# A two-layer decoder trunk on one core: program head reordered, attention outputs stored as split pairs, whole inputs re-read from DRAM, last attention later

## The chip, the core and the metric

One core of a Trainium2 chip runs the whole program in one launch. The engines have their own queues and run them strictly in order: PE (matrix products), DVE (vector), ACT (scalar activations, casts, and some DMA issues), POOL and SP (here mostly DMA issues). The time is the device time of the core in microseconds, median over runs. All data are float32.

## The reference, cut to what matters

Two residual layers over 512 tokens of width 2048. Layer 0 is gated differential attention, layer 1 is RWKV-7 time mixing; the change touches layer 0 alone, and the place where layer 1's first projection starts is not touched.

```python
hn = rms_norm(x, norm_w[0])
q, k, v, gate = jnp.split(hn @ w_in, 4, axis=-1)          # 8 heads, q and k: 2 x 128, v: 256
q = apply_rope(rms_norm(q, q_gain), cos, sin)
k = apply_rope(rms_norm(k, k_gain), cos, sin)
a = softmax(q0 k0) - lam * softmax(q1 k1)                 # causal, blocks of 128 queries
o = rms_norm(a @ v, subln_w) * (1.0 - lambda_init)
x = x + (o * silu(gate)) @ w_out
```

## The kernel before, in words

**Products in pairs.** A float32 operand is split into a high part (rounded to fp32r) and a low part (the rest), and a product is three fp32r products: high by high, high by low, low by high (`mm3`, L122). Weights are loaded as `wraw` tiles of 128x2x512 (512 KB); ACT casts the high part `wh` (L105), DVE subtracts for the low part `wl` (L106). The activations are kept transposed: `hH[k]`, `hL[k]`, 128 channels by 512 tokens, k from 0 to 15.

**Head 0** is computed plainly: `unit_tok` runs over eight weight pairs of 24 matmuls each, first for q and k (`qk0`), then for v and gate. While q and k of head 0 are computed, `make_h` (L1042, L1043) turns the rows of xT into `hH` and `hL` with the norm's weight; the token-wise factor 1/rms is applied later, to q, k and v. For that factor, ACT squares x (tile `junkx`, L822, 16 times 128x512, with sums), and DVE adds and takes the reciprocal root (`rsqrt`, lines 64 to 71). `copy_out` (L249) moves the four accumulators of `qk0` to the tiles `t1`; `head_qk` (L261 to L280) norms and rotates them; `turn_qk` (L295 to L299) transposes them in a chain of small steps.

**Heads 1 to 7** use a seven-product scheme on 2x2 blocks (`unit_head`, L544), for which `input_sums` prepares sums and differences of the halves of `h` once, during the v/gate unit of head 0 (S1, S2, S4) and after it (S3). Weight sums Ta, Tb, Tc are made by DMAs on POOL that accumulate into a loaded tile. The attention of head h-1 is cut into steps (a `Chain`) and put between the matmuls of head h, some matmuls apart; its output is transposed (`yt`, L387), scaled (L393) and stored to `yd` in DRAM (L394).

**The output projection** reads the attention outputs back as rows: `split_rows` loads rows 0 to 13 into the t1 tiles (`yr`, L441, on SP), ACT casts (L431) and DVE subtracts (L432). Rows 14 and 15 come straight from the attention of head 7, which is interleaved with the first of the projection's two plain column blocks. The other two column blocks use the seven-product scheme again.

**What sets the order.** The program is written in one order and a scheduler fixes the queue of every engine when the program is built: an instruction gets a priority from its place, `high_priority` moves it ahead, `issue_after` holds it until another one is placed. Nothing is reordered when it runs: what stands at the head of an engine's queue and waits, holds all that stand behind.

Of the kernel before, what the change touches and what calls it, by code (L numbers as in the profile page):

```python
# [34 lines left out]
class Ctx:  # L35
    pass

# [208 lines left out]
def copy_out(g, dst, ps):  # L246
    with g.tc.high_priority(offset=AHEAD):
        for d, p in zip(dst, ps):
            g.nc.scalar.copy(d, p[:])  # L249
# [76 lines left out]
def attention(g, h, qkT, qkL, sq, V, VL, G, gap, rows=None, keys=()):  # L326
# [57 lines left out]
    def turn_y(t):  # L384
# [5 lines left out]
        if rows is None:  # L390
            yT = w.tile([P, 2, P], F32, name="yTh", tag="yTh", bufs=1)
            for c in range(2):
                nc.scalar.activation(yT[:, c], pv[:, c], AF.Copy, scale=g.subw[:, c : c + 1])  # L393
            nc.scalar.dma_start(out=g.yd[h * 256 : (h + 1) * 256, ts].rearrange("(c p) t -> p c t", p=P), in_=yT[:])  # L394
            return
# [57 lines left out]
def input_sums(g, late):  # L453
# [301 lines left out]
def layer0(g, aps):  # L755
    nc, tc = g.nc, g.tc
    lx = ExitStack()
    g.lc = lx.enter_context(tc.tile_pool(name="lc0", bufs=1))
    with ExitStack() as cx:
# [76 lines left out]
        with tc.issue_after(g.made[-1][0]), tc.issue_after(g.made[-1][1]), tc.issue_after(masked):  # L836
# [5 lines left out]
    with ExitStack() as cx:  # L842
        g.work = cx.enter_context(tc.tile_pool(name="work", bufs=2))
        before = None
        for h in range(NH):
            if h:
                Chain(g, attention(g, h - 1, *before, 28 if h > 1 else 26, keys=rest), 20)
            t1s = [g.work.tile([P, 512], F32, name="t1", tag="t1", bufs=4) for _ in range(NT)]
# [12 lines left out]
            else:  # L861
                copy_out(g, [t[:] for t in t1s], qk0)
# [843 lines left out]
```

## Time and profile before

| | us |
|---|---|
| runs | 2154.02, 2154.74, 2157.23 (median 2154.74) |
| profiled execution, its own time | 2149.57 |
| its span, first to last instruction | 2147.8 |
| PE busy in it | 2107.1 (98%) |
| DVE, ACT, POOL busy | 1601.3 (75%), 1135.1 (53%), 361.6 (17%) |
| mean granted PE clock | 0.993 |

In the rows of a timeline the first number is the start, the second the busy time, then engine, line, operation, tiles and shapes; in brackets the idle time of the engine ahead of it and what ended it. In a table of windows each engine's busy time comes with the number of its instructions, then the granted PE clock, the share of the DMA engines that was busy, and GB/s.

### The profile page before, as it was taken

Reading aid. Unit: us, or ns where it says so; the run is one execution under the profiler, and the core shown is the slowest. Engines: PE = TensorE matmul, PEld = TensorE weight load, DVE = VectorE, ACT = ScalarE, POOL = GpSimd, SP = SyncE. Lnnn points to the kernel's source line nnn. Section 1 sums busy time; section 2 is a strip of 40 time slices with the busy share of each in tenths; the row PEclk is TensorE's granted clock in tenths of the full one; section 3 lists DMA queues with packets and bytes.
Section 4 is the critical chain, followed back from the end, with each engine's and each line's share of the span. In section 5 each row is a group of like instructions: output and inputs, shape, how many; then the busy total and the mean of one; then the engine's idle time right before and its main releaser. Section 6 shows DMA issues by size and latency. Waiting matters only on the chain.

```text
span 2147.8 us, 34089 instructions
## 1 busy us (share of the span) xinstructions
PE 2107.1 (98%) x11936; PEld 1712.8 (80%) x11936; DVE 1601.3 (75%) x4087; ACT 1135.1 (53%) x2265; POOL 361.6 (17%) x729
## 2 busy tenths in 40 slices
PE   9999999999999999999999999999999999999999
PEld 7788888888888788878676888788887887877887
DVE  5897888878788885575777778877777788766645
ACT  5565555655555453355554555565555555644322
POOL 1010101011011100101222222222222222221001
PEclk9999999999999999999999999999999999999999
DMA  8567767677676656723222322322332223336555
GB/s 273 142 140 180 167 156 180 156 186 157 167 186 162 175 193 195 173 76 105 79 79 77 94 84 92 93 89 87 94 96 92 89 87 95 111 115 186 178 164 120
DMA packets 132893, 288.32 MB, mean 134 GB/s; under 512 B 47232, under 2 KB 57472, under 8 KB 132720
## 3 DMA queue, kind: packets, MB, share of 16 engines
q1 hardware_dynamic: 75648, 187.46, 27.1%
q0 software_dynamic: 22048, 76.20, 18.5%
q10 hardware_dynamic: 35024, 22.46, 3.3%
q8 instruction: 94, 1.54, 0.3%
q14 instruction: 79, 0.65, 0.1%
HBM read 266.09 MB, written 19.99 MB: 133 GB/s over the span
## 4 chain that ended last, share of the span: by engine, by line
PE 69%; DVE 19%; issue 4%; DMA 4%; ACT 2%; POOL 0%; SPq 0%; ACTq 0%; DVEq 0%; POOLq 0%
PE pp L122 29%; PE pp L544 21%; PE pt L122 5%; DVE wl L106 4%; DVE tmpl L1305 3%; DVE Tm L1307 2%; DVE VS L1440 1%; PE sc L122 1%; PE gp L1241 1%; PE sm L1418 1%; DMA td<-Tm 1%; PE lora L122 1%; PE sm L1436 1%; DMA x<-in_x_dram 1%; PE o L122 1%
## 5 line engine op out<-in xcount | busy, mean ns | idle before, releaser
L106 DVE TENSOR_TENSOR wl<-wraw,wh 128x1024 fp32r<-128x1024 f32 (+2 forms) x305 | 371.3, 1217 | 233.1 <-ACT wh L105 220.1
L105 ACT CAST wh<-wraw 128x1024 fp32r<-128x1024 f32 (+2 forms) x305 | 318.3, 1044 | 342.9 <-PE pp L122 173.3
L122 PE MATMUL pp<-hH,wl 128*128 128x512 f32 x1024 | 415.4, 406 | 0.2 <-DVE wl L106 0.2
L122 PE MATMUL pp<-hL,wh 128*128 128x512 f32 x1024 | 415.2, 406 | 0.0
L122 PE MATMUL pp<-hH,wh 128*128 128x512 f32 x1024 | 412.7, 403 | 0.0
L122 PEld LDWEIGHTS pp<-hH,wh 128*128 128x128 f32 x1024 | 194.4, 190 | 35.9 <-issue 1.8
L122 PEld LDWEIGHTS pp<-hL,wh 128*128 128x128 f32 x1024 | 194.1, 190 | 34.9
L544 PE MATMUL pp<-wh,hH 128*128 128x512 f32 x560 | 220.8, 394 | 0.0
L122 PEld LDWEIGHTS pp<-hH,wl 128*128 128x128 f32 x1024 | 194.4, 190 | 33.1 <-DVE wl L106 0.7
L544 PE MATMUL pp<-wh,hL 128*128 128x512 f32 x560 | 218.7, 391 | 0.0
L544 PE MATMUL pp<-wl,hH 128*128 128x512 f32 x560 | 174.8, 394 | 0.1
L122 PE MATMUL pp<-wh,hH 128*128 128x512 f32 x372 | 147.5, 398 | 8.1 <-ACT t L249 3.3
L122 PE MATMUL pp<-wl,hH 128*128 128x512 f32 x372 | 148.0, 400 | 2.4 <-DVE wl L106 2.4
L122 PE MATMUL pp<-wh,hL 128*128 128x512 f32 x372 | 148.0, 399 | 0.2
L1305 DVE SCALAR_TENSOR_TENSOR tmpl<-LT,Tm 128x60 f32<-128x60 f32 (+24 forms) x496 | 134.8, 272 | 10.9
L1424 POOL COPY SA<-VS 64x64 f32<-64x64 f32 x224 | 60.9, 272 | 457.4 <-DVE VS L1440 354.9
L544 PEld LDWEIGHTS pp<-wh,hL 128*128 128x128 f32 x560 | 105.3, 188 | 21.4
L544 PEld LDWEIGHTS pp<-wh,hH 128*128 128x128 f32 x560 | 105.2, 188 | 21.0
L544 PEld LDWEIGHTS pp<-wl,hH 128*128 128x128 f32 x560 | 103.1, 188 | 21.9 <-DVE wl L106 0.8
L1307 DVE TENSOR_TENSOR Tm<-Tm,tmpl 128x60 f32<-128x60 f32 (+24 forms) x496 | 103.8, 209 | 11.2
L122 PEld LDWEIGHTS pp<-wh,hH 128*128 128x128 f32 x372 | 71.1, 191 | 24.0 <-ACT t L249 3.8
L1431 ACT COPY VS<-sm 64x64 f32<-64x64 f32 x256 | 52.7, 206 | 63.3 <-PE sm L1429 58.4
(384 smaller groups left out, 4233.9 us busy)
## 6 DMA issues: line engine op xcount, KB each, us to landing
wraw<-in_rw_w_in_dram SPq DMA_DIRECT2D x128, 512.0 KB
wraw<-in_da_w_in_dram SPq DMA_DIRECT2D x92, 512.0 KB
wraw<-in_da_w_out_dram SPq DMA_DIRECT2D x26, 512.0 KB
wraw<-in_rw_w_out_dram SPq DMA_DIRECT2D x26, 512.0 KB
Ta<-in_da_w_in_dram POOLq DMA_DIRECT2D x21, 512.0 KB, 5.4
Tb<-in_da_w_in_dram POOLq DMA_DIRECT2D x21, 512.0 KB, 5.9
Tc<-in_da_w_in_dram POOLq DMA_DIRECT2D x21, 512.0 KB, 5.8
wraw<-in_da_w_in_dram POOLq DMA_DIRECT2D x21, 512.0 KB, 5.4
```

The source lines that it names most:

```text
L105: a = nc.scalar.copy(hi[:, ks], raw[:, ks])
L106: d = nc.vector.tensor_sub(lo[:, ks], raw[:, ks], hi[:, ks].bitcast(F32))
L122: m = nc.tensor.matmul(out, a, b, start=s, stop=e, skip_group_check=skip)
L544: m = nc.tensor.matmul(out[t][:], x, wt[lo][:, k, :], start=first, stop=end and lo == 1 and k == KG - 1, skip_group_check=True)
L1241: m = nc.tensor.matmul(gp[h][:, i * P : (i + 1) * P], BK[r_, c0 + i, :, :], p.AR[r_, c0 + i, :, :], start=True, stop=True)
L1305: nc.vector.scalar_tensor_tensor(tt, LT[:, i : i + 1, i + 1 :].to_broadcast([P, s, n]), n2[:, i : i + 1], Tm[:, 0:s, i : i + 1].to_broadca ...
L1307: nc.vector.tensor_add(Tm[:, 0:s, i + 1 :], Tm[:, 0:s, i + 1 :], tt)
L1418: nc.tensor.matmul(sm[:, 0:P], both(p.G[:, c, 0]), both(VS[:, c]), start=True, stop=True)
L1424: nc.gpsimd.tensor_copy(p.SA[r_, c - 1, :], VS[r_, c, h, :])
L1431: nc.scalar.copy(VS[r_, c, h, :], sm[r_, P : P + C])
L1436: nc.tensor.matmul(sm[:, o : o + P], p.BKT[:, c, :], both(VS[:, c]), start=True, stop=True)
L1440: g.state = nc.vector.scalar_tensor_tensor(VS[r_, c + 1, h, :], s_, p.gam[r_, c : c + 1], Sg[r_, :], ALU.mult, ALU.add)
```

## The change

1. *Head 0.* The tiles `t1` get a pool of their own that outlives the program head, so `copy_out` of `qk0` is written right behind the q/k unit. The loads of x (four of 1 MB, on ACT's queue) are issued behind later rows of `make_h`, most squares behind the copies, and the computation of lambda too.
2. *Sums of the inputs.* `input_sums` no longer adds `hH+hL` on DVE. It loads the rows of xT once more (18 loads of 256 KB on POOL's queue) and applies the norm's weight in the operations that form the sums. The chain that transposes q and k of head 0 starts 104 matmuls on instead of 80.
3. *Attention outputs* are split when they are stored: per block of 128 channels a high part (ACT) and a low part (DVE), two stores per query block to `ys` instead of one to `yd`. Two DMAs on POOL per head form the whole values in `yd` from `ys`, one head later: a copy, then an accumulating one.
4. *Output projection.* Rows 0 to 13 are loaded from `ys` straight into `hH` and `hL` (28 loads of 256 KB on SP); L431 and L432 fall away there.
5. *Head 7.* Its v/gate ending has no raised priority any more, and its attention starts 16 matmuls after the unit's end instead of 4, with steps 20 instead of 21 matmuls apart.

```diff
+class Work:
+    def __init__(self, pool, heads):
+        self.pool, self.heads = pool, heads
+    def tile(self, *a, tag=None, **k):
+        return (self.heads if tag == "t1" else self.pool).tile(*a, tag=tag, **k)
...
         if rows is None:
-            yT = w.tile([P, 2, P], F32, name="yTh", tag="yTh", bufs=1)
             for c in range(2):
-                nc.scalar.activation(yT[:, c], pv[:, c], AF.Copy, scale=g.subw[:, c : c + 1])
-            nc.scalar.dma_start(out=g.yd[h * 256 : (h + 1) * 256, ts].rearrange("(c p) t -> p c t", p=P), in_=yT[:])
+                yT = w.tile([P, 2, P], F32R, name="yTh", tag=("yTh", "th")[c], bufs=1)
+                nc.scalar.activation(yT[:, 0], pv[:, c], AF.Copy, scale=g.subw[:, c : c + 1])
+                nc.vector.scalar_tensor_tensor(yT[:, 1], pv[:, c], g.subw[:, c : c + 1],
+                                               yT[:, 0].bitcast(F32), ALU.mult, ALU.subtract)
+                nc.scalar.dma_start(out=g.ys[2 * h + c, :, :, ts], in_=yT[:].bitcast(F32))
+            if h and t in (1, 3):
+                part, op = ((0, ALU.bypass), (1, ALU.add))[t // 2]
+                nc.gpsimd.dma_start(out=g.yd[(h - 1) * 256 : h * 256, :].rearrange("(c p) t -> c p t", p=P),
+                                    in_=g.ys[2 * h - 2 : 2 * h, :, part], accum_op=op)
             return
...
-    def whole(k, tag):
-        r = w.tile([P, T], F32, name="whole", tag=tag, bufs=1)
-        nc.vector.tensor_add(r[:], g.hH[k][:].bitcast(F32), g.hL[k][:].bitcast(F32))
+    def whole(r, k):
+        nc.gpsimd.dma_start(out=r, in_=aps["xT"][:, k])
         return r[:, 0:256], r[:, 256:512]
-    def put(nm, k, o, x, y, op):
-        nc.vector.tensor_tensor(out=o, in0=x, in1=y, op=op)
+    def put(nm, k, o, scale=1.0):
         hi, lo = g.sums[nm][k]
-        nc.scalar.copy(hi, o)
-        nc.vector.tensor_sub(lo, o, hi.bitcast(F32))
+        nc.scalar.activation(hi, o, AF.Copy, scale=scale)
+        nc.vector.scalar_tensor_tensor(lo, o, scale, hi.bitcast(F32), ALU.mult, ALU.subtract)
+    def mixed(o, x, scale, op):
+        nc.vector.scalar_tensor_tensor(o, x, scale, o, ALU.mult, op)
...
         if late:
-            a, b = whole(k, "a")
-            put("S3", k, b, a, b, ALU.subtract)
+            a, b = whole(w.tile([P, T], F32, name="whole", tag=("a", "at", "p0", "p1")[k % 4], bufs=1), k)
+            nc.vector.tensor_sub(a, a, b)
+            put("S3", k, a, norm(k))
             continue
-        (a, b), (c, d) = whole(k, "p0"), whole(k + NH4, "p1")
-        put("S1", k, d, b, d, ALU.subtract)
-        put("S2", k, d, d, a, ALU.subtract)
-        put("S4", k, c, c, d, ALU.add)
+        pair = w.tile([P, 2, T], F32, name="pair", tag=("V", "VL", "acc1", "G")[k % 4], bufs=1)
+        (a, b), (c, d) = whole(pair[:, 0], k), whole(pair[:, 1], k + NH4)
+        nc.scalar.activation(d, d, AF.Copy, scale=norm(k + NH4))
+        mixed(d, b, norm(k), ALU.subtract)
+        put("S1", k, d)
+        mixed(d, a, minus[:, k : k + 1], ALU.add)
+        put("S2", k, d)
+        nc.vector.scalar_tensor_tensor(c, c, norm(k + NH4), d, ALU.mult, ALU.add)
+        put("S4", k, c)
...
+        t1s = [t1_tile() for _ in range(NT)]
+        copied = copy_out(g, [t[:] for t in t1s], qk0)
...
-            with tc.issue_after(g.made[(2, 5, 8, 10)[cb]][0]):
+            with tc.issue_after(g.made[(7, 10, 13, 15)[cb]][0]):
...
-                with tc.issue_after(g.made[min(4 * cb + t + 6, KT - 1)][0]):
+                with tc.issue_after(g.made[12 + t][0] if cb == 0 else copied):
...
-                copy_out(g, [t[:] for t in t1s], qk0)
...
-                Chain(g, keys(NT), 80)
-                input_sums(g, False)
+                Chain(g, keys(NT), 104)
+                input_sums(g, aps, False)
...
-            with tc.high_priority(offset=AHEAD if h == NH - 1 else 0):
-                before = qkT + (sq,) + head_vg(g, h, vg, G)
+            before = qkT + (sq,) + head_vg(g, h, vg, G)
...
-        rows = split_rows(g, g.yd, ("t1",), 4, KT - 2, 8, g.gated)
-        ch = Chain(g, attention(g, h, *before, 21, rows, rest), 4)
+        rows = []
+        for k in range(KT - 2):
+            rows.append([g.hp.tile([P, T], F32R, name=n, tag=n) for n in ("hH", "hL")])
+            for i in range(2):
+                nc.sync.dma_start(out=rows[k][i][:].bitcast(F32), in_=g.ys[k, :, i])
+        ch = Chain(g, attention(g, h, *before, 20, rows, rest), 16)
...
+    g.ys = dr.tile([KT, P, 2, T], F32, name="ys")
-    g.yd = dr.tile([D, T], F32, name="yd")
+    g.yd = dr.tile([2 * NS * P, T], F32, name="yd")
```

How the queues move at three places. First ACT at the end of head 0's q/k unit, before (`COPY t<-pp` are the copies of `qk0`, `junkx` the squares of x, the number behind `x` the 1 MB load that they read, `wh<-wraw` the weight casts):

```order
L822 ACTIVATE junkx,ssc<-x_444 128x512
L239 ACTIVATE ls_579<-ls_579 128x1
L822 ACTIVATE junkx,ssc<-x_446 128x512 x2
L105 CAST wh<-wraw 128x1024
L822 ACTIVATE junkx,ssc<-x_446 128x512 x2
L249 COPY t_593<-pp 128x512
L249 COPY t_594<-pp 128x512
L249 COPY t_595<-pp 128x512
L249 COPY t_596<-pp 128x512
```

and in the change, from the first of the copies:

```order
L259 COPY t_445<-pp 128x512
L855 ACTIVATE junkx,ssc<-x_452 128x512
L222 ACTIVATE cs<-ang 128x256
L259 COPY t_446<-pp 128x512
L115 CAST wh<-wraw 128x1024
L855 ACTIVATE junkx,ssc<-x_452 128x512
L249 ACT_TABLE_LOAD
L249 ACTIVATE ls_583<-ls_583 128x1
L855 ACTIVATE junkx,ssc<-x_454 128x512
L249 ACTIVATE ls_591<-ls_591 128x1
L855 ACTIVATE junkx,ssc<-x_454 128x512 x2
```

The copies moved ahead of thirteen of the sixteen squares. Second, ACT further on, where the pairs of re-read rows are scaled, in the change (`pair` is the tile of two rows of xT, `squares` are those of q and k, whose 1/rms factor `rr` scales `t`, `sA` the high part of a sum):

```order
L272 ACTIVATE squares<-t_445,rstd_494 128x512
L517 ACTIVATE pair<-pair,norms 128x256
L272 ACTIVATE squares<-t_446,rstd_494 128x512
L517 ACTIVATE pair<-pair,norms 128x256
L115 CAST wh<-wraw 128x1024
L517 ACTIVATE pair<-pair,norms 128x256
L115 CAST wh<-wraw 128x1024
L498 ACTIVATE sA<-pair 128x256 x2
L291 ACTIVATE t_443<-t_443,rr 128x128 x2
```

The loads that these scalings wait for stand on POOL, right behind those of the program head:

```order
L872 DMA subw<-in_da_subln_w_dram 128x2x1
L493 DMA pair<-in_xT_dram 128x512 x8
L96 DMA Ta<-in_da_w_in_dram 128x1024
L96 DMA Tb<-in_da_w_in_dram 128x1024
L96 DMA Tc<-in_da_w_in_dram 128x1024
L493 DMA whole<-in_xT_dram 128x512 x4
L493 DMA pair<-in_xT_dram 128x512 x4
```

Before, no such row stood on either engine. Third, ACT between head 7's last products and the output projection, before (`hH<-yr` is a row of the attention output, `V` the values of head 7, `th` its gate):

```order
L298 CAST qkT<-pt 128x4x128
L431 CAST hH<-yr 128x512
L105 CAST wh<-wraw 128x1024
L298 CAST qkT<-pt 128x4x128
L431 CAST hH<-yr 128x512
L315 ACTIVATE V<-G,rstd_482 128x256
L317 ACTIVATE th<-G,hrstd_483 128x256
L315 ACTIVATE V<-G,rstd_482 128x256
L315 ACTIVATE V<-acc_6751,rstd_482 128x256
L105 CAST wh<-wraw 128x1024
```

and in the change:

```order
L309 CAST qkT<-pt 128x4x128
L115 CAST wh<-wraw 128x1024
L309 CAST qkT<-pt 128x4x128
L326 ACTIVATE V<-G,rstd_494 128x256
L328 ACTIVATE th<-G,hrstd_495 128x256
L326 ACTIVATE V<-G,rstd_494 128x256
L326 ACTIVATE V<-acc_6863,rstd_494 128x256
L115 CAST wh<-wraw 128x1024
```

The row casts left the queue; the weight cast and the copies of V follow each other.

More of the change, by code (lines that the diff above doesn't have):

```diff
@@ L248, in copy_out @@
         for d, p in zip(dst, ps):
-            g.nc.scalar.copy(d, p[:])
+            m = g.nc.scalar.copy(d, p[:])
+    return m.ins
 def head_qk(g, t1s, sq, ts):
@@ L450, with input_sums @@
 KG = 2
-def input_sums(g, late):
+def input_sums(g, aps, late):
     nc, w = g.nc, g.work
@@ L758, in layer0 @@
     g.lc = lx.enter_context(tc.tile_pool(name="lc0", bufs=1))
+    heads = lx.enter_context(tc.tile_pool(name="heads", bufs=4))
+    t1_tile = lambda: heads.tile([P, 512], F32, name="t1", tag="t1")
     with ExitStack() as cx:
@@ L835, in layer0 @@
                 rope_tables(g, aps)
-        with tc.issue_after(g.made[-1][0]), tc.issue_after(g.made[-1][1]), tc.issue_after(masked):
+        with tc.issue_after(copied), tc.issue_after(g.made[-1][1]), tc.issue_after(masked):
             lambda_full(g, aps)
@@ L842, in layer0 @@
     with ExitStack() as cx:
-        g.work = cx.enter_context(tc.tile_pool(name="work", bufs=2))
+        g.work = Work(cx.enter_context(tc.tile_pool(name="work", bufs=2)), heads)
         before = None
@@ L847, in layer0 @@
                 Chain(g, attention(g, h - 1, *before, 28 if h > 1 else 26, keys=rest), 20)
-            t1s = [g.work.tile([P, 512], F32, name="t1", tag="t1", bufs=4) for _ in range(NT)]
+            t1s = [t1_tile() for _ in range(NT)] if h else t1s
             sq = g.small.tile([P, NT, 2], F32, name="sq", tag="sq")
@@ L874, in layer0 @@
                     c.finish(g)
-                input_sums(g, True)
-            with tc.high_priority(offset=AHEAD if h == NH - 1 else 0):
-                before = qkT + (sq,) + head_vg(g, h, vg, G)
+                input_sums(g, aps, True)
+            before = qkT + (sq,) + head_vg(g, h, vg, G)
             if h == 0:
```

4 lines of the change are left out of this document (added).

## Prediction

> **What bounds the kernel now.** I read the page's first table, then the windows along the span, then the timeline of TensorE where a window loses time, and last the engine that it waited for.
>
> ```profile
> PE 2107.1 (98%) x11936; PEld 1712.8 (80%) x11936; DVE 1601.3 (75%) x4087; ACT 1135.1 (53%) x2265; POOL 361.6 (17%) x729
> ...
> core 0: us, PE busy (x) PEld busy (x) DVE busy (x) ACT busy (x) POOL busy (x), PEclk, DMA share, GB/s
> 0.00:50.00 50.00, 44.95 (x186) 35.77 (x187) 27.29 (x61) 28.04 (x49) 7.07 (x17) 0.97 0.88 284
> 50.00:100.00 50.00, 46.66 (x206) 37.90 (x205) 43.72 (x143) 27.30 (x55) 2.65 (x3) 0.97 0.51 147
> 400.00:450.00 50.00, 49.82 (x242) 41.53 (x241) 41.91 (x122) 29.11 (x54) 7.64 (x9) 1.00 0.77 164
> 700.00:750.00 50.00, 45.56 (x206) 36.85 (x204) 39.92 (x91) 25.05 (x39) 6.06 (x9) 0.99 0.68 179
> 750.00:800.00 50.00, 49.10 (x233) 39.71 (x234) 39.87 (x136) 28.07 (x63) 2.83 (x4) 0.94 0.62 200
> ```
>
> TensorE sets the time: 2107.1 of 2147.8 us, so all its idle time is 40.7 us. The change removes no matmul, so it can win only idle time, and the slow clock that follows. In a steady head (400 to 450) only 0.18 us is idle: nothing is to be had there, only lost. The head of the program, the end of head 7 and the output projection are what the edit touches, and there the timeline shows these stalls:
>
> ```profile
> 20.88 0.50 PE L122 MATMUL pp<-wh,hH 128*128 128x512 f32 x1 [2.52 <-ACT hH L1042]
> ...
> 59.47 0.50 PE L122 MATMUL pp<-wh,hH 128*128 128x512 f32 x1 [3.33 <-ACT t L249]
> 59.81 0.48 PE L122 MATMUL pp<-wl,hH 128*128 128x512 f32 x1
> 60.09 0.63 PE L122 MATMUL pp<-wh,hL 128*128 128x512 f32 x1
> ...
> 63.45 0.39 PE L122 MATMUL pp<-wl,hH 128*128 128x512 f32 x1
> 63.68 0.40 PE L122 MATMUL pp<-wh,hL 128*128 128x512 f32 x1
> ...
> 746.68 0.50 PE L122 MATMUL pp<-wh,hH 128*128 128x512 f32 x1 [1.83 <-DVE acc L508]
> ...
> 749.84 2.08 PE L122 MATMUL pp<-wl,hH 128*128 128x512 f32 x4 [2.44 <-DVE wl L106]
> 752.39 0.47 PE L295 MATMUL pt<-ident,t 128*128 128x128 f32 x1 [0.47 <-ACT t L280]
> ...
> 769.90 0.44 PE L363 MATMUL pt<-ident,a 128*128 128x128 f32 x2 [0.33 <-DVE rs_i L64]
> ```
>
> A stall is paid twice. After 3.33 us idle, the eight matmuls from 60.09 to 63.45 stand 0.42 us apart, against 0.23 from 63.45 on: about 1.5 us more for one slow stretch. The windows show the same clock:
>
> ```profile
> 60.00:64.00 4.00, 4.00 (x12) 3.09 (x11) 3.18 (x14) 2.59 (x5) 0.00 (x0) 0.58 0.92 335
> 750.00:756.00 6.00, 5.53 (x14) 3.85 (x15) 3.86 (x10) 2.37 (x6) 0.00 (x0) 0.50 0.79 231
> ```
>
> The Trainium skill ("TensorE: Matmul & The Clock Gate", Part 1) has the clock fall back after an idle window of 3413 ns. By that rule a stall of 2.5 us costs only itself; the sum below would then count idle time alone and come to -2.8 instead of -5.0. The trace is stricter than the page: the 2.44 us stall already stands before six microseconds at 0.50.
>
> **The change, part by part.** The sum is made against the profiled execution, 2149.57 us (its span 2147.8 and 1.8 around it); it lies 5.2 under the median of the runs, 2154.74, to which I apply the difference.
>
> *1. Copy-out of head 0.* Let E be the end of head 0's q/k unit, 56.14 (59.47 less the stall). Before, the four copies stood behind all 16 squares:
>
> ```profile
> 57.12 0.62 ACT L822 ACTIVATE junkx<-x 128x512 f32<-128x512 f32 x1
> 57.66 0.19 ACT L822 ACTIVATION_READ_ACCUMULATOR junkx<-x 128x1 f32 x1
> 57.88 0.63 ACT L822 ACTIVATE junkx<-x 128x512 f32<-128x512 f32 x1
> 58.41 0.19 ACT L822 ACTIVATION_READ_ACCUMULATOR junkx<-x 128x1 f32 x1
> 58.83 2.05 ACT L249 COPY t<-pp 128x512 f32<-128x512 f32 x4 [0.23 <-DVE ss L823]
> ```
>
> Now each copy follows its own accumulator. The 3.33 us stall goes, with its 1.5 us of slow clock: -4.8.
>
> *2. x loads later.* The stall at 20.88 waits for a row of xT while x shares the engines.
>
> ```profile
> q1 hardware_dynamic: 212, 0.77, 62.8%
> q10 hardware_dynamic: 175, 0.36, 30.7%
> ```
>
> These are the queues of SyncE and ScalarE from 18 to 21 us; all queues moved 1.13 MB in those 3 us. Without the 0.36 MB the rest is there some 0.9 us earlier (estimate, 0.36 MB at that rate). I take -0.9; bounds 0 and -4.0 (the whole stall with its slow stretch).
>
> *3. What is late next.* Thirteen squares now follow E instead of two. At 0.75 us each (57.12 to 57.88), with three weight casts, the table load and two copies among them, they end near E+15 (before: E+2.5). The sum over them and the reciprocal root on DVE took from here to here:
>
> ```profile
> 58.63 0.17 DVE L823 TENSOR_REDUCE ss<-ssc 128x4 f32<-128x16 f32 x1 [0.15 <-ACT junkx L822]
> ...
> 61.90 0.16 DVE L71 SCALAR_TENSOR_TENSOR rstd<-rs_t,rs_i 128x4 f32<-128x4 f32 x1
> ```
>
> That is 3.4 us, so E+18.5. The squares, rotations and second root of q/k follow; the first scaled t1 can be there at E+33 at the earliest, and the static order of TensorE wants its transpose 140 matmuls after E, at E+31.8. So 1.4 us is lost even if every load is early.
>
> *4. Pair loads.* The halves that DVE rebuilt from hH+hL now come from DRAM by twelve 256 KB loads on POOL's queue, whose memory is free only when the last square is done (E+15). ScalarE scales four of them in front of the weight casts of the sixth and seventh group, needed at E+27.3 and E+32.9. What such a load takes, in the rows nearest:
>
> ```profile
> L896 POOL DMA_DIRECT2D xq<-in_x_dram x8: 707/794/881, 683.3 to 715.2; - x8
> ...
> DMA to landing us min/median/max: 5.8/7.9/9.0
> ...
> LT<-ltd POOLq DMA_DIRECT2D x64, 132.0 KB, 2.8
> ```
>
> xq is the same 256 KB form on the same queue, issued 0.7 apart. With 5.8 to 7.9 to landing, the third pair (sixth load, issued near E+18.6) is there at E+24.4 to 26.5. One scaling (0.4), the cast (1.05) and the weight's low half (1.2) follow: E+27.1 to 29.2 against E+27.5. Stall 0 to 1.7, I take 1.0. It pushes the DVE chain of t1 behind it: 1.4 to 3.0 there, I take 2.0. Pairs five and six use the buffers of one and two again, so their loads leave only after the sums of pair one, 6.8 us after the scaled t1; ScalarE has them in front of the copies that free the accumulators for the next unit. With 3.5 to 6 us to landing the copy ends 0.4 to 3.9 late; I take 2.0, nearer to LT, as little else moves then. Together 5.0 (1.8 to 8.6), and one or two slow stretches, 2.3 (0 to 4.5). The first stage thus gives back what it wins: -4.8 -0.9 +7.3 = +1.6.
>
> For such a load the Trainium skill ("DMA: Bandwidth & Descriptors", Anatomy of one DMA) fits 2.0 us plus bytes over 436 GB/s, 2.6 us here as an estimate. LT's 2.8 us agrees, xq's 5.8 at the least does not. By the page the pairs would all be early: that is the first rival below.
>
> *5. Output projection.* Here ScalarE stood still for a row of yd, with V's copies behind it, and the DVE behind those:
>
> ```profile
> 744.07 0.62 ACT L431 CAST hH<-yr 128x512 fp32r<-128x512 f32 x1 [4.29 <-DMA yr<-yd]
> 744.60 0.50 ACT L315 ACTIVATE V<-G,rstd 128x256 fp32r<-128x256 f32 x1
> ...
> 745.13 0.48 DVE L318 SCALAR_TENSOR_TENSOR VL<-G,rstd,V 128x256 fp32r<-128x256 f32 x1 [1.52 <-ACT V L315]
> 745.95 0.68 DVE L508 TENSOR_TENSOR acc<-acc,pp 128x512 f32<-128x512 f32 x1
> 748.57 1.22 DVE L106 TENSOR_TENSOR wl<-wraw,wh 128x1024 fp32r<-128x1024 f32 x1
> ```
>
> The 14 casts (0.62) and 14 subtractions are gone, the 28 row loads sit on SyncE alone, and the accumulators and low halves are now ahead of V's work on DVE. Behind the last matmul of head 7 (T) DVE has one accumulation (0.68) and a low half (1.22) left, needed 0.7 us after T: 0.3 of stall, and about 0.7 more where the scaled t1 and the second block's scores are tight. The rows are 7.3 MB; SyncE may start them 27 us before T as slots come free. At 0.40 MB/us (the 401 GB/s of the window 22 to 26 below) they need 18 us and are wanted over the 50 us after T. So 5.07 us of stall becomes 1.0, and the two slow stretches (750 to 756, half of 6 us) go: -4.1 -3.0 = -7.1. Bounds -8.0, and -3.0 if one stall of 2 us stays.
>
> ```profile
> 22.00:26.00 4.00, 4.00 (x12) 3.11 (x11) 0.98 (x2) 1.78 (x3) 0.00 (x0) 0.57 1.03 401
> ```
>
> *6. Steady heads.* Each head gets eight more DVE operations of 128x128, four more stores, two DRAM-to-DRAM moves ahead of Tc on POOL. ScalarE was idle 21 of 50 us and Tc's first matmul stands 160 matmuls behind its new place (at 0.23 us, 36 us). I take +0.5 in all; bounds 0 and +3.
>
> Sum: +1.6 -7.1 +0.5 = -5.0: 2144.6 for the profiled execution, **2149.7** for the median.
>
> **The rivals.** *Loads land early* (LT's 2.8 us scaled, or the page's 2.6): the first stage keeps only the 1.8 us of stalls that lateness of the squares forces, without slow clock; -3.9 there, -10.5 in all, 2144. For it: POOL's queue is otherwise empty. Against it: Ta, Tb and Tc (1.5 MB) start on the same release. *Loads late as xq's 9.0*: 8.6+4.5 instead of 7.3, +0.8 in all, 2155.5. *Rows late*: the fourth weight of the projection stands behind row 12 on SyncE; if it comes 4 us late, with a slow stretch, part 5 falls to -1.6: +0.5, 2155. *The stores hold ScalarE* (slower): each store now waits for a DVE low half in the DVE's own order, which may have a 1.22 us weight half in front, 56 times; the weight casts stand behind it on ScalarE. It decides once a cast is late by more than its lead: at 0.3 us each it is 17 us, +11, 2166. For it: the steady heads have no slack on TensorE; against: ScalarE has 21 us of 50.
>
> **How the numbers follow.** Forecast 0.40 (from -8 to -2, a little more than half of it beyond 0.2%), early loads 0.25, late loads 0.12, late rows 0.08, stores 0.15. A difference of 0.2%, 4.3 us, is what a measurement of this kernel can tell. Faster: 0.25 of the early loads and 0.25 of the forecast, 0.50. Same: the forecast's other 0.15, late loads and late rows, 0.35. Slower: 0.15. The range is 2142.5 (early loads with a little of part 2's bound) to 2160 (late loads with part 6's bound); the forecast's own is 2146.5 to 2153.
>
> **What would show it.** Right: no stall at E; stalls near E+27, E+32 to 36 and E+45 to 50 that name pair loads or t scaled; in the output projection no L431-like idle on ScalarE, and PEclk near 1.00 for six microseconds after T. Wrong: a first stage without stalls after E; low-half or cast stalls spread over the heads; more than 0.3 us idle in a window of 50 there; matmuls of the projection that wait for hH rows.

## The result, and the profile after

The changed kernel takes **2192.2 us** (median of four runs, 2190.8 to 2199.79) against 2154.85 before: 1.0178 times as long, 95% interval 1.0156 to 1.0199. Forecast was 2149.7, range 2142.5 to 2160.

Three starts on TensorE cut the first layer into stages: the first matmul with form S1 (`pp<-wh,sA`) in head 1, the same in head 7, and the first transposition of layer 1 (`xT<-ident,xq`). The first layer is what the change touches, so everything behind the third start is code that both kernels share. From the timeline of TensorE of the kernel before:

```profile
127.87 1.08 PE L544 MATMUL pp<-wh,sA 128*128 128x512 f32 x4
...
674.89 0.63 PE L544 MATMUL pp<-wh,sA 128*128 128x512 f32 x2
...
929.66 0.44 PE L981 MATMUL xT<-ident,xq 128*128 128x128 f32 x2 [0.57 <-DVE xq L948]
```

and of the kernel after, with the stalls between them (heads 2 to 7 all have the pair shown for heads 5 and 7):

```profile
20.30 0.50 PE L132 MATMUL pp<-wh,hH 128*128 128x512 f32 x1 [1.64 <-ACT hH L1077]
...
85.12 0.50 PE L132 MATMUL pp<-wh,hH 128*128 128x512 f32 x1 [2.47 <-ACT wh L115]
86.38 0.66 PE L132 MATMUL pp<-wl,hH 128*128 128x512 f32 x1 [0.76 <-DVE wl L116]
94.15 0.33 PE L306 MATMUL pt<-ident,t 128*128 128x128 f32 x1 [1.60 <-ACT t L291]
...
108.57 0.50 PE L573 MATMUL pp<-wh,hH 128*128 128x512 f32 x1 [0.66 <-ACT acc L259]
128.09 0.30 PE L374 MATMUL pt<-ident,a 128*128 128x128 f32 x1 [1.78 <-DVE a L368]
131.69 1.08 PE L573 MATMUL pp<-wh,sA 128*128 128x512 f32 x4
...
522.13 0.74 PE L573 MATMUL pp<-wh,sA 128*128 128x512 f32 x2 [1.62 <-ACT wh L115]
533.81 2.07 PE L573 MATMUL pp<-wh,sA 128*128 128x512 f32 x4 [3.68 <-ACT wh L115]
...
720.49 0.74 PE L573 MATMUL pp<-wh,sA 128*128 128x512 f32 x2 [1.62 <-ACT wh L115]
732.18 1.22 PE L573 MATMUL pp<-wh,sA 128*128 128x512 f32 x2 [3.68 <-ACT wh L115]
...
974.58 0.44 PE L1016 MATMUL xT<-ident,xq 128*128 128x128 f32 x2 [0.60 <-DVE xq L983]
```

| stage of the profiled execution | before | after | difference |
|---|---|---|---|
| up to head 1's S1 | 127.87 | 131.69 | +3.8 |
| head 1's S1 to head 7's | 547.02 | 588.80 | **+41.8** |
| head 7's S1 to layer 1 | 254.77 | 254.09 | -0.7 |
| layer 1 (to the span's end) | 1218.1 | 1223.4 | +5.3 |

The program head and the projection went nearly as forecast; the six steady heads did not. One row of the groups by line says it, the matmuls with S1: before,

```profile
L544 PE MATMUL pp<-wh,sA 128*128 128x512 f32 x168 | 46.9, 393 | 0.0
```

and after:

```profile
L573 PE MATMUL pp<-wh,sA 128*128 128x512 f32 x168 | 53.5, 436 | 31.8 <-ACT wh L115 31.8
```

31.8 us is six times 1.62 + 3.68. Head 7's 3.68 lies behind the second of the three starts, so the stage of +41.8 holds six of the short stalls and five of the long ones, 28.1 us. Each long stall is followed by 3.4 us at half the clock, 1.7 us of loss, or 8.5 for the five; the short ones are not. The remaining 5.2 us I did not take apart: cast_late below loses 0.3 us per stall besides its idle time, and the heads of rows_add lose 2.8 us without any of these stalls. Windows of the kernel after around one head's two stalls (busy time by engine, then granted clock):

```profile
521.00:525.00 4.00, 2.87 (x15) 2.56 (x16) 3.72 (x11) 2.40 (x4) 0.60 (x1) 1.00 0.00 0
533.70:537.10 3.40, 3.29 (x10) 2.61 (x10) 2.36 (x2) 1.33 (x3) 0.84 (x1) 0.50 0.21 26
```

What TensorE waits for there is the cast of a weight sum on ScalarE. Before, Ta's cast runs ahead of the copy that frees an accumulator (`t<-pp`), and Tc's ahead of the output scaling and its store. ScalarE, before:

```profile
580.12 1.05 ACT L105 CAST wh<-Ta 128x1024 fp32r<-128x1024 f32 x1 [0.66 <-ACT p L349]
581.89 0.58 ACT L249 COPY t<-pp 128x512 f32<-128x512 f32 x1 [0.72 <-PE pp L544]
...
588.62 1.04 ACT L105 CAST wh<-Tc 128x1024 fp32r<-128x1024 f32 x1
...
590.96 0.44 ACT L376 ACTIVATE o<-o,r 128x256 f32<-128x256 f32 x1
```

ScalarE, after:

```profile
518.83 0.59 ACT L259 COPY t<-pp 128x512 f32<-128x512 f32 x1 [2.43 <-PE pp L573]
...
520.54 0.58 ACT L259 COPY t<-pp 128x512 f32<-128x512 f32 x1 [0.66 <-PE pp L573]
521.03 1.05 ACT L115 CAST wh<-Ta 128x1024 fp32r<-128x1024 f32 x1
...
529.55 0.45 ACT L387 ACTIVATE o<-o,r 128x256 f32<-128x256 f32 x1 [1.40 <-PE o L132]
...
532.15 0.52 ACTq L407 DMA_DIRECT2D ys<-yTh  x1
532.71 1.04 ACT L115 CAST wh<-Tc 128x1024 fp32r<-128x1024 f32 x1 [0.98 <-DVE rs_t L79]
```

Now Ta's cast stands behind both copies, and a copy can only start when TensorE has finished the unit: ScalarE idles 2.43 us for it, TensorE then idles 1.62 us for the cast. Tc's cast stands behind the scalings and two stores, which wait for the attention's last matmul and for DVE. No data is late: the addition that completes Ta is issued 30 us before the cast, at 490.83, that of Tc 33 us before, at 500.04, and such additions land in 5.7 and 7.9 us (medians). POOL, after, with the two moves between the additions:

```profile
474.58 0.60 POOL L410 DMA_DIRECT2D yd<-ys  x1 [7.61 <-DMA ys<-yTh]
490.83 0.85 POOL L96 DMA_DIRECT2D Ta<-in_da_w_in_dram  x1 [15.65 <-DVE qkL L310]
...
499.46 1.23 POOL L410 DMA_DIRECT2D yd<-ys  x1
500.04 1.56 POOL L96 DMA_DIRECT2D Tc<-in_da_w_in_dram  x1
```

The projection nearly kept its promise. Its start lies some 45 us later here, in the windows from 750 to 850: 0.54 us idle and the clock at 1.00, where the windows from 700 to 800 before had 5.34 us idle and 0.99 and 0.94. Further on, at 874.18, one new stall of 1.29 us waits for a low half (`wl`).

```profile
750.00:800.00 50.00, 50.00 (x230) 40.89 (x229) 42.80 (x97) 24.35 (x38) 6.42 (x9) 1.00 1.00 297
800.00:850.00 50.00, 49.46 (x249) 40.70 (x248) 38.15 (x130) 24.84 (x57) 2.84 (x4) 1.00 0.52 179
```

### The profile page after: what moved, and what is told of

Read it like the earlier page. It is cut to its first block, busy times and chain, and to the rows that moved or that the text cites. A ratio compares the mean times of both kernels' runs of the same rounds, so it can differ in the third digit from the quotient of the medians.

```text
span 2198.0 us, 34234 instructions
## 1 busy us (share of the span) xinstructions
PE 2122.9 (97%) x11936; PEld 1717.2 (78%) x11936; DVE 1607.2 (73%) x4112; ACT 1133.2 (52%) x2257; POOL 379.8 (17%) x759
## 4 chain that ended last, share of the span: by engine, by line
PE 65%; DVE 16%; issue 6%; DMA 5%; ACT 3%; POOL 1%; ACTq 0%; SPq 0%; POOLq 0%; DVEq 0%
PE pp L132 26%; PE pp L573 21%; PE pt L132 5%; DVE wl L116 3%; DVE tmpl L1340 3%; DVE Tm L1342 2%; DVE VS L1475 1%; DMA td<-Tm 1%; ACT wh L115 1%; PE gp L1276 1%; PE sc L132 1%; PE sm L1453 1%; DMA Ta<-in_da_w_in_dram 1%; DMA TT<-td 1%; PE lora L132 1%
```

## The experiments

My theory after the comparison: the place of the weight casts in ScalarE's fixed order costs the time, and the twelve moves on POOL displaced them (place theory). The rival is the one of the prediction, that the split stores hold ScalarE (stores theory). In the expectations "planner" is the scheduler that fixes the queues. The column "S1 idle" is TensorE's idle time ahead of `pp<-wh,sA`, as in the rows above; "layer 1" is the start of `xT<-ident,xq`.

| run | ratio to before (95%) | S1 idle, us | layer 1 starts |
|---|---|---|---|
| before | 1 | 0.0 | 929.7 |
| after | 1.0178 (1.0156 to 1.0199) | 31.8 | 974.6 |
| head_only | 1.0006 (0.9990 to 1.0023) | 0.0 | 932.8 |
| out_only | 1.0187 (1.0163 to 1.0211) | 32.2 | 973.1 |
| movelate | 1.0253 (1.0229 to 1.0278) | 9.7 | 986.1 |
| held_moves | 1.0102 (1.0077 to 1.0127) | 0.0 | 958.2 |
| moves_only | 1.0193 (1.0173 to 1.0213) | 11.8 | 979.8 |
| sp_stores | 1.0238 (1.0216 to 1.0261) | 21.8 | 979.0 |
| acc_behind | 1.0122 (1.0086 to 1.0158) | 0.0 | 952.0 |
| head_early | 1.0009 (0.9994 to 1.0024) | 0.0 | 927.6 |
| cast_late | 1.0057 (1.0035 to 1.0080) | 11.3 | 943.2 |
| no_moves | 1.0094 (1.0079 to 1.0109) | 0.0 | 951.9 |
| no_moves_early | 1.0063 (1.0046 to 1.0080) | 0.0 | 944.9 |
| rows_add | 0.9993 (0.9978 to 1.0009) | 0.0 | 931.2 |
| rows_add_early | 0.9971 (0.9955 to 0.9988) | 0.0 | 929.0 |

### Which half

**head_only** has edits 1 and 2 of the change, **out_only** edits 3 to 5.

> Parts 1 and 2 of the change alone (program head, re-read inputs); stores, output projection and last attention as before. Both theories on the heads (the place of the casts of Ta and Tc in ScalarE's order; the split stores themselves) expect no stall in heads 1 to 6, since neither the order there nor the stores change, and the stalls of 746 to 752 us as before. In the first stage the changed kernel idled 8.9 us (20.30, 85.12, 86.38, 94.15, 108.57, 128.09) against 6.3 before (6.44, 20.88, 59.47), with two slow stretches in both: 2155 to 2160 us. If the stall at 128.09 belongs to parts 3 to 5, 1.8 less.

> Parts 3 to 5 alone (split stores, moves in DRAM, projection's rows loaded, last attention later) on the kernel before. Both theories expect the two stalls of every head, 1.62 and 3.68 us, with or without a slow stretch of 1.5 behind the longer: 6 x 5.3 = 32 to 6 x 7.0 = 42 more, and the projection's 7 less: 2180 to 2190 us.

Measured: 2155.78 against 2155.69 for the head alone, 2194.64 for the outputs alone (some 5 above the expected range), which show the same two stalls in heads 2 to 7 (S1 idle 32.2). So the loss is in the outputs' half. In head_only the stall at 59.47 is gone and others have come, 6.7 us together:

```profile
83.32 0.50 PE L132 MATMUL pp<-wh,hH 128*128 128x512 f32 x1 [1.79 <-ACT wh L115]
84.58 0.53 PE L132 MATMUL pp<-wl,hH 128*128 128x512 f32 x1 [0.76 <-DVE wl L116]
92.35 0.33 PE L306 MATMUL pt<-ident,t 128*128 128x128 f32 x1 [1.57 <-ACT t L291]
106.78 0.50 PE L567 MATMUL pp<-wh,hH 128*128 128x512 f32 x1 [0.67 <-ACT acc L259]
126.40 0.30 PE L374 MATMUL pt<-ident,a 128*128 128x128 f32 x1 [1.87 <-DVE a L368]
```

### The moves elsewhere

**movelate** writes the twelve moves behind head 7, where the scheduler is still free to place them earlier; **held_moves** also holds them behind POOL's last weight addition (`g.added`; the line with it is in held_moves alone).

```diff
-            if h and t in (1, 3):
-                ...
+        for h0 in range(NS):
+            for part, op in ((0, ALU.bypass), (1, ALU.add)):
+                with tc.issue_after(g.added):
+                    nc.gpsimd.dma_start(out=g.yd[h0 * 256 : (h0 + 1) * 256, :].rearrange("(c p) t -> c p t", p=P),
+                                        in_=g.ys[2 * h0 : 2 * h0 + 2, :, part], accum_op=op)
```

> The changed kernel with its twelve moves from ys to yd written behind head 7 instead of inside the attention; they still find a place on POOL in the heads, but Tc's load is then ahead of the second one. In ScalarE's order the cast of Tc stands ahead of the output block and its stores again, the cast of Ta still behind the two copies. All 56 stores stay. Place of the casts: the 3.68 us stall and its slow stretch go, the 1.62 us stall stays: 2192 less 6 x 3.7 to 6 x 5.2, 2161 to 2170 us. Stores themselves: no change, 2185 to 2195 us.

> The changed kernel with its twelve moves held on POOL until the last weight addition of head 7; POOL's loads in the heads and ScalarE's casts of Ta, Tb and Tc then stand as before the change. All 56 stores stay. Place of the casts: both stalls of every head go: 2192 less 6 x 5.3 to 6 x 6.8, 2151 to 2160 us, unless the 12 moves (6.3 MB) collide with the projection's rows, which would show as stalls of TensorE after 740 us. Stores themselves: 2185 to 2195 us.

movelate took 2209.42, a miss for both theories' numbers, though not for what it tells. The scheduler put the moves back into the heads, one ahead of Ta, one behind Tc. Tc's stall went, Ta's stayed, and a third cast, of the form S2, fell behind stores and scalings:

```profile
465.63 2.08 PE L569 MATMUL pp<-wh,sB 128*128 128x512 f32 x4 [4.49 <-ACT wh L115]
```

In held_moves (2175.81) heads 2 to 7 show no such stall (S1 idle 0.0) although all 56 split stores stand there. That alone is against the stores theory. The time went elsewhere: twelve moves in a row occupy the DMA engines, which are busy throughout from 740 to 780 (share 1.07), when the projection's weights are due (ScalarE), and hold the loads of whole rows (POOL), which are issued only at 796.24. Head 7 has one stall of 2.29 us besides, at 703.86, which waits for the tile of the split stores (`yTh`). ScalarE, then TensorE:

```profile
780.36 1.04 ACT L115 CAST wh<-wraw 128x1024 fp32r<-128x1024 f32 x1 [13.39 <-DMA wraw<-in_da_w_out_dram]
```

```profile
781.62 0.58 PE L132 MATMUL o<-V,at 128*128 128x256 f32 x1 [8.49 <-ACT at L377]
...
876.69 0.76 PE L132 MATMUL pp<-wh,hH 128*128 128x512 f32 x1 [10.60 <-ACT fS L669]
```

### Moves without stores, and stores without moves

**moves_only** is the kernel before with two moves per head into a scratch tensor:

```diff
+            if h and t in (1, 3):
+                op = (ALU.bypass, ALU.add)[t // 2]
+                nc.gpsimd.dma_start(out=g.ye[2 * h - 2 : 2 * h, :, 0],
+                                    in_=g.yd[(h - 1) * 256 : h * 256, :].rearrange("(c p) t -> c p t", p=P), accum_op=op)
```

> The kernel before with nothing but two 256 KB moves from DRAM to DRAM per head added on POOL (into a scratch tensor that nothing reads), with its whole stores, its 28 row casts and its program head unchanged. No split store is in it. Place theory (the moves change where the planner puts the weight casts in ScalarE's order; here only Ta's cast goes behind the copies of t and a scaling): one stall of about 1.6 us on ScalarE's wh in every head from the second on, none of 3.7, and with a slow stretch of up to 1.7 us each: 2164 to 2175. Stores theory (the split stores hold ScalarE): nothing is added to ScalarE, so no stall in the heads: 2154 to 2158. Traffic theory (6 to 14 us of extra load on the shared DMA engines makes the weights land late): stalls whose releaser is a wh or wl that itself waits for a DMA of Ta, Tb or Tc.

Measured 2197.35: moves alone, without one split store, make the kernel as slow as the whole change, so such a loss needs no split store. Ta's stall of 1.62 is there as expected in six heads (S1 idle 11.8, with one more of 2.04 in head 2). In five of the heads a second stall, of 3.19 to 4.68, adds more than the place theory's sum allowed for, so the time is no proof of that theory; the stall has a part of the traffic theory in it, a cast that waits for a DMA, but by way of a queue. (The moves are of 512 KB each, not 256 as the expectation says.) A move stands between Tb's addition and Tc's on POOL and waits 4.00 us for the store that it copies, with Tc's addition behind it; ScalarE then waits 8.02 us for Tc, and TensorE 4.66. From the timelines of POOL, ScalarE and TensorE:

```profile
366.04 0.60 POOL L397 DMA_DIRECT2D ye<-yd  x1 [4.00 <-DMA yd<-yTh]
366.63 0.88 POOL L86 DMA_DIRECT2D Tc<-in_da_w_in_dram  x1
```

```profile
376.15 1.04 ACT L105 CAST wh<-Tc 128x1024 fp32r<-128x1024 f32 x1 [8.02 <-DMA Tc<-in_da_w_in_dram]
```

```profile
377.25 0.72 PE L548 MATMUL pp<-wh,hH 128*128 128x512 f32 x1 [4.66 <-ACT wh L105]
```

So a move has two ways to cost time: it goes with a later place of casts, and it holds POOL's queue. In the changed kernel only the first shows: the move that waits 7.61 us at 474.58 has no addition behind it until 490.83, and the one at 499.46 doesn't wait.

**sp_stores** is the changed kernel with `nc.sync.dma_start` for the stores to `ys`.

> The changed kernel with its 56 split stores issued by SyncE instead of ScalarE; the moves stay where they are on POOL. In ScalarE's order Tc's cast then stands behind one scaling of yTh and no store, Ta's cast still behind the copies of t. Place theory: the 1.62 us stall of each head stays, the 3.68 one goes or falls under 1.5: 2192 less 6 times 3.7 to 5.4, 2160 to 2172. Stores theory (the waits of the stores on ScalarE are the cost, wherever the casts stand): both stalls go, 2152 to 2158. If stores that wait on SyncE hold the weight loads queued behind them there: new stalls on wh with a DMA of wraw behind them, above 2192.

Measured 2206.23. Tc's cast now stands behind the two scalings alone and its stall falls from 3.68 to about 2.0, not under 1.5 as the place theory had it; a low half then stalls for 1.4 more, and the clock falls as before (0.57 in the 4 us behind). The stores in front of the cast were thus worth 1.7 us of its stall, the place behind the scalings the rest. Ta's 1.62 stays in heads 2 to 7. The stores theory, by which both stalls should go, fails here as it did in held_moves; the time for the whole is a miss for both, and why it is 14 us above that of the changed kernel is not shown.

**acc_behind** keeps the stores, stores the high half once more straight into `yd`, and needs one accumulating move per head, held on POOL behind the third addition of the head after next.

```diff
+                if h < NS:
+                    nc.scalar.dma_start(out=g.yd[(2 * h + c) * P : (2 * h + c + 1) * P, ts], in_=yT[:, 0].bitcast(F32))
...
+                if h > 1:
+                    with tc.issue_after(g.added[2]):
+                        nc.gpsimd.dma_start(out=g.yd[(h - 2) * 256 : (h - 1) * 256, :].rearrange("(c p) t -> c p t", p=P),
+                                            in_=g.ys[2 * h - 4 : 2 * h - 2, :, 1], accum_op=ALU.add)
```

> The changed kernel with the split stores, all on ScalarE, and the high half stored once more, straight into the place where the whole value is to be, so that one accumulating move per head (six in all) is enough; it is held on POOL behind the third weight addition of the head after next. With that the casts of Ta, Tb and Tc stand in ScalarE's order where they stood before the change. Place theory: no stall over 0.5 us in heads 1 to 6 although 56 split stores, 48 further stores and 6 moves are there; stage 1 as in the changed kernel (+1 to +3 against before), projection as in the changed kernel (-7): 2149 to 2154. Stores theory: the stalls stay in every head, 2190 or more. Traffic theory: accumulating moves of 6 to 14 us stand ahead of the additions of wraw, so new stalls on wh or wl of wraw in every head: 2160 to 2175.

Measured 2179.44. The casts ahead of S1 are back in their places and S1 idle is 0.0 with split stores in every head and six moves: the two stalls go with the place. But each of heads 2 to 7 has two other stalls: 1.02 to 3.05 us for `yTh`, and 0.66 to 1.68 for a weight cast ahead of plain products (`pp<-wh,hH`). I put the first down to my extra store, since `yTh` has one buffer and two DMAs now read it before it may be written again; the forecast of 2149 to 2154 missed both:

```profile
339.50 0.66 PE L374 MATMUL pt<-ident,a 128*128 128x128 f32 x4 [2.14 <-DVE yTh L405]
```

### One cast alone

**cast_late** is the kernel before with one line of order: Ta's cast for S1 may not start ahead of the copy of the second pair of accumulators.

```diff
-    copy_out(g, q[:2], y)
+    copied = copy_out(g, q[:2], y)
     X = pair()
     for i in range(N):
-        products(X, form("S1", i), split(g.Ts[i]), i == 0)
+        with g.tc.issue_after(copied) if i == 0 else ExitStack():
+            wt = split(g.Ts[i])
+        products(X, form("S1", i), wt, i == 0)
```

> The kernel before with one thing moved: in every head from the second on, the cast of Ta for the first form with S1 may only start behind the copy that frees the second pair of accumulators, which is where it stands in the changed kernel. No split store, no move, no other edit. Place theory: a stall of 1.6 us on ScalarE's wh in each of seven heads, 11.3 us, and up to 1.7 us of slow clock behind each: 2166 to 2178. If the place does not matter and the moves themselves (their traffic, or POOL's queue behind them) cost the time: 2154 to 2158.

Measured 2168.45, 12.2 us more, with exactly the predicted stall in all seven heads:

```profile
L545 PE MATMUL pp<-wh,sA 128*128 128x512 f32 x168 | 47.7, 398 | 11.3 <-ACT wh L105 11.3
```

From head 1's S1 to head 7's it takes 558.58 (129.44 to 688.02), 11.56 more than before: six stalls (9.72) and 1.8 besides. This stall brings no slow clock. The place of a cast costs time with neither stores nor moves. This run moves Ta's cast alone; Tc's, behind the longer stall, I did not move alone. For it there are two other runs: in movelate, with all stores, it stands ahead of the output block again and its stall goes, and in sp_stores it stands behind the scalings without stores and 2.0 us stay.

### The change without its moves

**no_moves** lets the projection add the halves while it loads whole rows, by six plain and six accumulating loads from `ys`; **no_moves_early** has besides the loads of x and the squares as early as before. **head_early** does that to head_only.

```diff
-            with tc.issue_after(g.made[(7, 10, 13, 15)[cb]][0]):
+            with tc.issue_after(g.made[(2, 5, 8, 10)[cb]][0]):
...
-                with tc.issue_after(g.made[12 + t][0] if cb == 0 else copied):
+                with tc.issue_after(g.made[min(4 * cb + t + 6, KT - 1)][0]):
```

> The program head alone, with head 0's copies directly behind their accumulators as in the change, but with the loads of x and the squares as early as before the change (so two or three squares are left after the unit's end instead of 13); heads, stores and projection as before the change. If the late squares gave back what the copies won (part 3 of the prediction): the 3.33 us stall at 59.5 goes with its slow stretch, the stalls near 83 to 107 (1.8, 0.8, 1.6, 0.7) shrink to under 2 together: 2149 to 2152. If the pair loads of input sums alone give it back (part 4), the stalls near 83 to 92 stay: 2154 to 2157.

> The changed kernel without its twelve moves: the 56 split stores stay on ScalarE, and the output projection adds the halves as it loads them (the high half by a plain load, the low half by an accumulating load into the same tile, six of each). POOL then has nothing more to do in the heads than before the change, and the casts of Ta, Tb and Tc stand where they stood. Place theory, and what the moves cost: no stall over 0.5 us in heads 1 to 6; the first stage gives back what it wins (+1 to +3 in the trace), the projection keeps its gain (-7), less what the six longer loads cost there (0 to 3): 2149 to 2155. Stores theory: as the changed kernel, 2185 or more.

> The same without moves, with the loads of x and the squares of the program head as early as before the change. The first stage then keeps its gain (3.33 us of stall at the end of head 0's unit and its slow stretch, less about 1.9 of new stalls, as in the program head alone with early squares, where the first layer ended 2.0 earlier), unless the pair loads, now behind earlier squares and beside other stores, stall anew. With the projection's -7: 2146 to 2151. If the second layer's own spread (its span differs by 6 us between executions of the same code) hides it, the interval will hold 1 and only the time at which the first layer ends shows the gain.

no_moves, 2175.17 where 2149 to 2155 was expected, has heads 1 to 6 without a stall over 0.5 us, as held_moves had, and one of 2.43 for `yTh` in head 7. It pays 14 us in the projection: the loads' tiles come free only with the last attention, and sums and weight halves wait behind them on DVE and ScalarE.

```profile
819.94 0.76 PE L132 MATMUL pp<-wh,hH 128*128 128x512 f32 x1 [8.42 <-ACT fS L673]
...
849.39 0.79 PE L132 MATMUL pp<-wl,hH 128*128 128x512 f32 x1 [5.62 <-DVE wl L116]
```

no_moves_early (2170.12, expected 2146 to 2151) starts layer 1 7.0 earlier than no_moves, and head_early 5.2 earlier than head_only. In the medians head_early (2156.94, expected 2149 to 2152) shows nothing: its layer 1 starts 2.0 earlier than before in the trace, but the interval of 0.9994 to 1.0024 does not hold such a gain. In the profiled execution layer 1 took 7.4 us more than that of before, with the same code.

**rows_add** drops whole values in DRAM altogether: where the projection's sums need one, DVE adds the two halves that lie in SBUF. **rows_add_early** has the early squares too.

```diff
+            for k in range(KG):
+                with g.tc.issue_after(g.rowsplit):
+                    nc.vector.tensor_add(r[:, k], src[0][k0 + k][:].bitcast(F32), src[1][k0 + k][:].bitcast(F32))
```

> The changed kernel without moves and without the whole values in DRAM: where the projection's sums need a whole value, DVE adds the two halves that lie in SBUF anyway, 12 additions of 128x512 (0.69 us each, 8 us on an engine that is half idle there). Everything else as in the changed kernel, the 56 split stores included. If the moves alone make the change slower: no stall over 0.5 us in heads 1 to 6, one of about 2.4 in head 7, stage 1 as in the changed kernel, and the projection without stalls of 8.4 and 5.6 us; the first layer ends 2 to 6 us earlier than before the change (929.7), and the whole takes 2149 to 2156. If the split stores have a price of their own: the first layer ends at 930 to 940, 2156 to 2166.

> The same with the loads of x and the squares of the program head as early as before the change. If the late squares gave back what the early copies won: the stalls from 85 to 128 (2.4, 0.8, 1.8, 0.6, 1.6) become about 1.9 together and the first layer ends 5 us earlier than in the run with late squares and 6 to 12 earlier than before the change: 2144 to 2151, an interval that lies below 1. If the pair loads stall anyway: like the run with late squares.

rows_add takes 2153.95 against 2155.28: the rest of the change, all 56 split stores included, costs nothing in sum that can be measured, nor does it win. The time is as expected; layer 1, though, starts 1.5 later than before and not 2 to 6 earlier. Its stages, by the same three starts:

```profile
132.82 1.08 PE L569 MATMUL pp<-wh,sA 128*128 128x512 f32 x4
...
682.64 0.62 PE L569 MATMUL pp<-wh,sA 128*128 128x512 f32 x2
...
931.18 0.44 PE L1017 MATMUL xT<-ident,xq 128*128 128x128 f32 x2 [0.56 <-DVE xq L984]
```

Up to head 1 it loses 5.0, in the heads 2.8 (549.82 for 547.02), behind them it wins 6.2 (248.54 for 254.77), though that stage holds a stall of 1.52 for `yTh` at 703.80. rows_add_early gets the program head back (its head 1 starts S1 at 125.67) and loses some of it in the heads (554.26), so that layer 1 starts 2.2 earlier than in rows_add where 5 was expected. At 2150.71 against 2155.28 it is the only version that beats the kernel before, by 0.3% (0.12 to 0.45%).

## Why the prediction was wrong, by its steps

**Part 6, the steady heads, is the step that failed.** It gave +0.5 us, bounds 0 and +3, on the ground that ScalarE has 21 of 50 us to spare and that Tc's first matmul stands 36 us behind its new place on POOL. Measured: +41.8. Tc was indeed in time, and so was ScalarE's sum of work. What I did not ask is in which order ScalarE does it: the twelve moves made the scheduler put the casts of Ta and Tc behind instructions that wait for TensorE, so that TensorE waits for itself. Both orders were there to be read before any run. cast_late shows the price of Ta's place alone (11.3 us of idle time), held_moves, no_moves and rows_add that both stalls go when the moves leave the heads, moves_only that moves bring Ta's stall without split stores. Why the scheduler answers an added move with a later cast was not tested.

**The rival "stores hold ScalarE"** had the right sign, the right engine and the right victim (a weight cast), for +11. Its cause falls: with 56 split stores and no moves in the heads, S1 idle is 0.0. What the stores cost by themselves is about the 2.8 us of rows_add's heads, inside the bounds that part 6 gave, the 1.52 us for `yTh` in head 7, and a share of Tc's stall where its cast stands behind them (1.7 of 3.68).

**Part 1** is right: the 3.33 us stall at the end of head 0's unit goes, and its slow stretch too. **Part 2** is right in size here (2.52 became 1.64, -0.9), but that is luck: with the same order of loads the wait for xT is 2.16 in head_only and 3.41 in rows_add, a spread larger than the term.

**Parts 3 and 4** were forecast at 5.0 of stalls by pair loads and late t1. The four stalls that they name took 5.5 (2.47, 0.76, 1.60, 0.66). The pair loads took 4.1 to 11.1 us to landing, 9.0 in the median, nearer to the rival of late loads than to the 5.8 to 7.9 of the sum; LT's 2.8 us, which the prediction set beside them, is for 132 KB and not 256. (The wait for t1 in part 3, "1.4", is 1.2 by its own two times, E+33 and E+31.8.) A fifth was missed, 1.78 ahead of a transposition of `a` at 128.09: head 0's attention starts on the delayed q and k. The stage came to +3.8 for a forecast +1.6. head_early says whose fault it is. With early squares three stalls are left, of 0.17, 0.76 and 1.10, and the pair loads are issued 9 us earlier (from 61.0, in the changed kernel from 70.0). So the pair loads are late because their memory waits for the late squares, as part 4 had it.

**Part 5** is right: -7.1 was forecast, -6.2 measured behind head 7's S1 in rows_add, or -7.7 without the wait for `yTh`, with no stall over 0.25 us between 703.8 and layer 1. In the changed kernel itself head 7's second stall and its slow clock (3.68 + 1.7) and the 1.29 at 874.18 stand in the same stage and leave -0.7.

**The clock.** I had read from the 2.44 us stall that any stall of some 2 us is paid twice. The traces do not bear that out, nor any rule by length alone. In the heads the clock stays at 1.00 behind the 1.62 us stalls and halves behind 3.68 (and behind 4.66 in moves_only). It halves too around two stalls close together, 2.02 + 1.39 with 1.2 us of matmuls between them in sp_stores; and the 2.44 us stall of before had one of 1.83 just ahead of it, 4.27 us together. But at the first wait for xT, near 20 us, single stalls of 1.64 (after) and 2.52 (before) are followed by a slow stretch, and 2.16 (head_only) and 2.60 (head_early) are not. The window from 21.70 to 25.10, first in the kernel after, then in head_early, whose stall is the longer:

```profile
21.70:25.10 3.40, 3.40 (x10) 2.69 (x9) 1.85 (x3) 2.28 (x3) 0.00 (x0) 0.50 1.03 416
...
20.95 0.50 PE L132 MATMUL pp<-wh,hH 128*128 128x512 f32 x1 [2.60 <-ACT hH L1068]
...
21.70:25.10 3.40, 3.36 (x15) 2.76 (x16) 0.65 (x1) 0.94 (x1) 0.00 (x0) 1.00 1.04 404
```

The Trainium skill ("TensorE: Matmul & The Clock Gate", Part 1) has the clock fall after an idle window of 3413 ns; the 1.64 and the 2.52 us show that less can do. What decides between 1.6 and 2.6 us is open.

**The medians** differ by 37 us, the profiled executions by 50: the one of before lay 5.2 under its median, as the prediction said, and that of after 7.6 above.

## What to carry to other kernels

Where queues are fixed when the program is built, an added DMA is not only its own cost: compare, on every engine, the order of what the bottleneck waits for (here the casts), ahead of any sum of busy times. Here the weight casts had to stand ahead of the instructions that wait for the bottleneck itself. And before values go through DRAM to be added, look whether both halves lie in SBUF anyway: 12 additions on a half-idle engine replaced 12 moves, and rows_add is 38 us faster than the changed kernel.

## What the runs showed that I had not expected

The second layer, the same code in all kernels, took between 1217.2 us (held_moves) and 1227.4 us (head_only, sp_stores) from its first transposition to the end of the profiled span. That is a spread of 10 us, more than most of the effects looked for here. Between these ends it is the clock that the traces record: layer 1 stands 10.2 us at half of it in held_moves and 30.7 us in head_only and sp_stores, and 20.5 us at half the clock cost 10.2 us. Why the slow stretches fall differently is open. So stages are better compared by their starts than by whole times; but a gain of 2 us at the start of layer 1 comes from one trace, and for head_early the medians of ten runs did not confirm it.

Moves from DRAM to DRAM were slow in the changed kernel: the 512 KB ones land in 10.7 us (median) where an accumulating load of the same size takes 5.7 to 7.9. That is no property of the size, since those of moves_only, also 512 KB, land in 6.3 us (median). From the list of DMA issues of the kernel after, 400 to 600 us (KB each, median us to landing):

```profile
Tc<-in_da_w_in_dram POOLq DMA_DIRECT2D x7, 512.0 KB, 7.9
...
yd<-ys POOLq DMA_DIRECT2D x5, 512.0 KB, 10.7
```
